# Norms without GpSimd, their roots and products in PSUM, and the squared ReLU in PSUM

## The chip, the cores and the metric

The kernel runs on one core of one Trainium2 chip. The metric is the device time of one execution in microseconds (us). Five engines matter: PE (TensorE, matmuls), DVE (VectorE), ACT (ScalarE), POOL (GpSimd) and SP (SyncE, whose queue issues all transfers). SBUF is the working memory; PSUM, eight banks of 512 fp32 columns, takes PE's results and can be read and written by DVE and ACT.

## What is computed

Two layers of a diffusion trunk work on 1024 latent tokens and 256 context tokens of width 1024. Cut to what matters here:

```python
def rmsnorm(x, g):
    y = xf * lax.rsqrt(jnp.mean(xf * xf, axis=-1, keepdims=True) + EPS)
    return y.astype(x.dtype) * g
h = rmsnorm(x, g_pre_mix) * (1 + sc1) + sh1          # "modulate"
y = concat(short conv, latent attention, conformer conv, 2-D attention)(h @ w_in) @ w_out
x = x + ga1 * rmsnorm(y, g_post_mix)                 # "norm"
hm = rmsnorm(x, g_pre_mlp) * (1 + sc2) + sh2         # "modulate"
x = x + ga2 * rmsnorm(square(relu(hm @ w1)) @ w2, g_post_mlp)   # "norm"
```

## The kernel before

Features lie on the 128 partitions (8 tiles `k`), tokens on the free axis, in three segments: 0 and 1 of 512 latent tokens, 2 of 256 context tokens. Every product is kept to fp32 accuracy by three matmuls on a high and a low part (`mm3`, L119 to L126). A weight block is loaded raw, ACT rounds it to the high part `wh`, and POOL or DVE subtracts to get the low part `wl` (L96 to L109); `walt` says how many of four go to DVE.

`rstd` (L153 to L174) makes the root of a norm: matmuls with ones sum the squares (L163), ACT takes the square root, DVE the reciprocal (L167) and a diagonal (L169), a matmul broadcasts it to all partitions (L172), and ACT copies it from PSUM into SBUF (L173). `norm` (L200 to L233) multiplies the result `y` by gain and root on DVE (L221, in place in SBUF, two SBUF inputs), adds the residual `xl` (L223: of four groups two on DVE, two on POOL), stores it, and squares and folds it (L227, L150) for the next root. `modulate` (L176 to L195) multiplies by gain and root (L188, in place), rounds the high part with its shift on ACT (L189) and makes the low part on DVE (L194), for every third `k` by an extra ACT pass and a subtraction on POOL (L191, L192).

PSUM tiles have tags: S with 3 banks, G with 2, T with 2, O with 1. A request for "R" is dealt a tag by `self.rot`: "G" means two banks turn, `ROT1 = 'SGSGS'` five, `ROT2 = 'SGSGO'` six. Attention uses S, T and O; so does the long convolution (T, O). While the attention of the later segments runs beside the first segment's MLP, `rot` is "G" (L995), and it stays so until that MLP reaches its tail and the attention is drained (L1027 to L1029).

The order of work is written out by generators: each yields a cost, and `merge` (L948) advances side work by a rate from `RATES` while the main work goes on; what is merged is issued in that order, and a scheduler with a cost model then places it on the engines' in-order queues. In `layer` (L967) the output projection of segment 1 goes in two halves, with the norm of the first half beside the second (`pn`), the norm of the second beside the context's projection (`pm`) and so on, then the MLP of segments 1 and 2. In `mlp` phase 1 makes two hidden tiles (L891, ReLU on ACT L893, square on DVE L894, high and low part), phase 2 adds eight products into the accumulators (L923).

Of the kernel before, what the change touches and what calls it, by code (L numbers as in the profile page):

```python
# [28 lines left out]
LOP = 3  # L29
PA, PB, PC, PD, PE_ = 0, 0, 1, 1, 0  # L30
DADD = (1, 3)
WALT = (3, 2)
MPE, RM, MX = 7, 1.0, 4
ROT0, ROT1, ROT2 = 'SGSGS', 'SGSGS', 'SGSGO'
# [12 lines left out]
def f32(ap):  # L47
    return ap.bitcast(F32)
# [15 lines left out]
class Kern:  # L64
# [88 lines left out]
    def rstd(self, accs, width, n, ptag, tag="e2"):  # L153
# [22 lines left out]
    def modulate(self, get, n, l, which, v, H, o, acc=None, ptag="R", tag="e2"):  # L176
# [5 lines left out]
        rs = self.rstd([acc], D, n, ptag, tag)  # L182
        yield n / 100
        A, sh = self.gains(l, "A" + which, v), self.gains(l, "s" + which, v)
        for k in range(KT):
            x = get(k)
            hi, lo = (h.k(k)[:, o:o + n] for h in (H() if callable(H) else H))
            nc.vector.scalar_tensor_tensor(x, x, A[:, k:k + 1], rs, op0=ALU.mult, op1=ALU.mult)  # L188
            nc.scalar.activation(hi, x, AF.Identity, bias=sh[:, k:k + 1])  # L189
            if k % LOP == LOP - 1:  # L190
                nc.scalar.activation(x, x, AF.Identity, bias=sh[:, k:k + 1])  # L191
                nc.gpsimd.tensor_tensor(lo, x, f32(hi), op=ALU.subtract)  # L192
            else:
                nc.vector.scalar_tensor_tensor(lo, x, sh[:, k:k + 1], f32(hi), op0=ALU.add, op1=ALU.subtract)  # L194
            yield n / 400  # L195
# [4 lines left out]
    def norm(self, y, si, o, n, l, which, acc, xsrc, xdst, nxt=None, ptag="R", tag="e2"):  # L200
# [12 lines left out]
        rs = self.rstd([acc], D, n, ptag, tag)  # L213
# [655 lines left out]
    def mlp(self, l, segs, H, atag, gtags, ends, ready=None):  # L869
# [7 lines left out]
        def phase1(b):  # L877
# [8 lines left out]
            def one(W, i, si, o, n):  # L886
# [7 lines left out]
                nc.vector.tensor_tensor(r, r, r, op=ALU.mult)  # L894
# [72 lines left out]
    def layer(self, l, H, pend):  # L967
# [45 lines left out]
        attb = ch(*[self.mla_attend(h, bsegs) for h in range(NH)], *[self.na_attend(l, h, bsegs) for h in range(NH)])  # L1013
# [263 lines left out]
```

## Time and profile before

| | us |
|---|---|
| median of 3 runs (lowest to highest) | 3301.18 (3299.84 to 3304.88) |
| profiled execution | 3295.16 |
| its span on the core | 3293.1 |
| PE busy | 2989.4 (91%) |
| DVE busy | 2150.5 (65%) |
| ACT busy | 1421.3 (43%) |
| POOL busy | 1190.5 (36%) |

The span is what the profiler's records cover; the profiled execution's own time is 2.1 us longer. Shares of busy time are averages over stages with different limits, so a stage is read by itself. TensorE's granted clock was 0.952 of full speed on the mean.

### The profile page before, as it was taken

How to read it: one execution, taken by the hardware profiler on the slowest of the kernel's cores; microseconds unless marked ns; L12 is line 12 of the kernel's file. 1: busy time of each engine (PE TensorE's matmuls, PEld its weight loads, DVE VectorE, ACT ScalarE, POOL GpSimd, SP SyncE). 2: the span in 40 equal slices, each digit the busy share in tenths (PEclk: the TensorE clock that was granted, in tenths of full speed). 3: DMA queues.
4: the chain of work that ended last, by engine and by line, in shares of the span. 5: the costliest groups of instructions: out<-in, count | busy, mean ns of one | idle time of the engine just before them, and what ended most of it. 6: DMA issues, size and time to landing. Idle time of an engine off the chain costs nothing.

```text
span 3293.1 us, 46055 instructions
## 1 busy us (share of the span) xinstructions
PE 2989.4 (91%) x15916; PEld 2552.7 (78%) x15916; DVE 2150.5 (65%) x4062; ACT 1421.3 (43%) x2933; POOL 1190.5 (36%) x927
## 2 busy tenths in 40 slices
PE   6779889879999979989999788998989999989997
PEld 5677668878877877878888577777878877877886
DVE  8999456675754487985645788557776644665445
ACT  3323455665643454213322433555665433543332
POOL 2402212234544444323333531222334444345444
PEclk9889889989999989989999899998989999999998
DMA  6435423543532354573222433425445322434233
GB/s 242 150 123 191 114 61 112 144 128 110 158 99 93 120 160 136 179 227 99 84 64 64 129 129 116 142 73 143 147 112 146 107 93 93 154 104 140 95 96 102
DMA packets 284461, 410.01 MB, mean 125 GB/s; under 512 B 28098, under 2 KB 129474, under 8 KB 284228
## 3 DMA queue, kind: packets, MB, share of 16 engines
q1 hardware_dynamic: 284228, 407.07, 40.1%
q8 instruction: 126, 2.06, 0.3%
q14 instruction: 107, 0.88, 0.1%
HBM read 354.66 MB, written 52.30 MB: 124 GB/s over the span
## 4 chain that ended last, share of the span: by engine, by line
PE 41%; DVE 12%; DMA 3%; ACT 2%; issue 2%; SPq 0%; POOL 0%; DVEq 0%; ACTq 0%; POOLq 0%
PE G L124 7%; PE G L125 7%; PE G L126 7%; PE S L124 4%; PE S L125 4%; PE S L126 4%; DMA xl<-in_wmodt_dram 2%; DVE T L400 2%; DVE xl L286 1%; PE T L673 1%; DVE ac L923 1%; DVE ac L221 1%; PE O L124 1%; PE O L125 1%; PE O L126 1%
## 5 line engine op out<-in xcount | busy, mean ns | idle before, releaser
L96 POOL TENSOR_TENSOR wl<-raw,wh 128x512 fp32r<-128x512 f32 x672 | 924.5, 1379 | 1434.5 <-ACT wh L95 1378.4
L95 ACT ACTIVATE wh<-raw 128x512 fp32r<-128x512 f32 x768 | 481.7, 629 | 798.3 <-PE G L125 357.0
L124 PE MATMUL G<-h,wh 128*128 128x512 f32 (+1 forms) x1296 | 488.9, 378 | 13.8 <-ACT wh L95 5.8
L125 PE MATMUL G<-h,wh 128*128 128x512 f32 (+1 forms) x1296 | 484.6, 374 | 5.2 <-DVE h L194 5.2
L126 PE MATMUL G<-h,wl 128*128 128x512 f32 (+1 forms) x1296 | 484.2, 374 | 2.4 <-POOL wl L96 2.4
L894 DVE TENSOR_TENSOR ge<-ge 128x512 f32<-128x512 f32 (+1 forms) x168 | 186.7, 1113 | 357.3 <-ACT ge L893 356.9
L923 DVE TENSOR_TENSOR ac<-ac,G 128x512 f32<-128x512 f32 (+1 forms) x370 | 236.8, 641 | 119.6 <-PE G L126 118.5
L124 PEld LDWEIGHTS G<-h,wh 128*128 128x128 f32 x1296 | 247.8, 191 | 58.0 <-ACT wh L95 7.1
L657 POOL TENSOR_SCALAR ah<-ah,sm 128x1280 f32<-128x1280 f32 (+3 forms) x144 | 150.0, 1045 | 380.3 <-DVE sm L656 161.6
L124 PE MATMUL G<-s,wh 128*128 128x512 f32 (+1 forms) x732 | 268.3, 368 | 17.3 <-DVE ac L923 9.1
L126 PEld LDWEIGHTS G<-h,wl 128*128 128x128 f32 x1296 | 247.7, 191 | 46.3 <-POOL wl L96 4.6
L125 PEld LDWEIGHTS G<-h,wh 128*128 128x128 f32 x1296 | 247.8, 191 | 45.8 <-DVE h L194 5.6
L126 PE MATMUL G<-s,wl 128*128 128x512 f32 (+1 forms) x732 | 261.8, 358 | 7.1 <-DVE wl L96 7.1
L125 PE MATMUL G<-s,wh 128*128 128x512 f32 (+1 forms) x732 | 261.5, 357 | 0.3 <-DVE s L96 0.3
L124 PE MATMUL S<-h,wh 128*128 128x512 f32 (+1 forms) x648 | 236.6, 365 | 3.2 <-DVE pt L96 2.6
L96 DVE TENSOR_TENSOR pt<-T,pt 128x512 fp32r<-128x512 f32 (+1 forms) x280 | 169.7, 615 | 98.7 <-ACT pt L95 97.4
L125 PE MATMUL S<-h,wh 128*128 128x512 f32 (+1 forms) x648 | 233.9, 361 | 0.0
L126 PE MATMUL S<-h,wl 128*128 128x512 f32 (+1 forms) x648 | 232.3, 359 | 1.1 <-POOL wl L96 1.1
L95 ACT ACTIVATE pt<-T 128x512 fp32r<-128x512 f32 (+1 forms) x280 | 146.7, 542 | 112.7 <-PE T L673 97.5
L673 PE MATMUL T<-ident,ah 128*128 128x128 f32 x976 | 164.8, 287 | 15.6 <-POOL ah L657 15.6
L124 PEld LDWEIGHTS G<-s,wh 128*128 128x128 f32 x732 | 139.9, 192 | 46.9 <-DVE ac L923 19.2
L400 DVE SCALAR_TENSOR_TENSOR T<-c,vec,T 128x512 f32<-128x512 f32 x240 | 169.4, 743 | 0.0
(372 smaller groups left out, 6990.8 us busy)
## 6 DMA issues: line engine op xcount, KB each, us to landing
raw<-in_w_dram SPq DMA_DIRECT2D x520, 256.0 KB, 2.6
xl<-in_wmodt_dram SPq DMA_DIRECT2D x160, 256.0 KB, 2.9
raw<-in_wout_dram SPq DMA_DIRECT2D x144, 256.0 KB, 2.9
raw<-in_win_dram SPq DMA_DIRECT2D x96, 256.0 KB, 3.1
ah<-KN SPq DMA_DIRECT2D x32, 320.0 KB, 4.7
ah<-MV SPq DMA_DIRECT2D x16, 640.0 KB, 6.4
ah<-NV SPq DMA_DIRECT2D x16, 640.0 KB, 5.2
XM<-yo SPq DMA_DIRECT2D x36, 256.0 KB, 2.7
```

What stands on the lines that cost most here:

```text
L95: nc.scalar.activation(hi, src, AF.Copy)
L96: (eng or nc.vector).tensor_tensor(lo, src, f32(hi), op=ALU.subtract)
L124: nc.tensor.matmul(out, wh, xh, start=i == 0, stop=False)
L125: nc.tensor.matmul(out, wh, xl, start=False, stop=False)
L126: nc.tensor.matmul(out, wl, xh, start=False, stop=i == last)
L221: nc.vector.scalar_tensor_tensor(yk(j), yk(j), B[:, j:j + 1], rs, op0=ALU.mult, op1=ALU.mult)
L286: nc.vector.scalar_tensor_tensor(q, w, 1.0, vecs[v][h], op0=ALU.mult, op1=ALU.mult, accum_out=dst)
L400: nc.vector.scalar_tensor_tensor(d, x, w, d, op0=ALU.mult, op1=ALU.add)
L657: nc.gpsimd.tensor_scalar(p[:, :L], p[:, :L], sm[:, 9:10], 1.0, op0=ALU.mult, op1=ALU.mult)
L673: nc.tensor.transpose(T[:, i, q * P:(q + 1) * P], ps_list[q][:, cols[q]:cols[q] + P], self.ident)
L894: nc.vector.tensor_tensor(r, r, r, op=ALU.mult)
L923: nc.vector.tensor_tensor(a, a, ps, op=ALU.add)
```

## The change

It takes the POOL instructions out of `modulate` and `norm`, so that all of their elementwise work is on DVE. `rstd` can leave its result in PSUM (`keep`, when its bank is O), and then makes no copy. With `tmp="T"` the products of L188 and L221 go to a T bank, from which the high and low parts, or the residual add, read. All norms get this but those of segment 0 beside attention, which stay in place and only lose POOL; the first segment's MLP norms and its modulates get `tmp="T"` with a rotated bank for the root. The sixth bank leaves `ROT2`. A one-step generator `turn` at the end of the attention of the later segments sets `rot` to `ROT1` as soon as that attention has been issued. In `mlp`, unless `rot` is "G", the square is written over the PSUM tile. In `layer` the norm of segment 1's first half gets the rate 1.5 in both layers (before: 0.612 in layer 0, 1.5 in layer 1) and is issued to its end before the second half's norm begins.

```diff
-ROT0, ROT1, ROT2 = 'SGSGS', 'SGSGS', 'SGSGO'
+ROT0, ROT1, ROT2 = 'SGSGS', 'SGSGS', 'SGSGS'
...
         nc.tensor.matmul(ps[:, :n], self.ones, s, start=True, stop=True)
+        if keep:
+            return ps[:, :n]
         nc.scalar.activation(s, ps[:, :n], AF.Copy)
...
-        rs = self.rstd([acc], D, n, ptag, tag)
+        rs = self.rstd([acc], D, n, ptag, tag, ptag == "O")
...
-            nc.vector.scalar_tensor_tensor(x, x, A[:, k:k + 1], rs, op0=ALU.mult, op1=ALU.mult)
-            nc.scalar.activation(hi, x, AF.Identity, bias=sh[:, k:k + 1])
-            if k % LOP == LOP - 1:
-                nc.scalar.activation(x, x, AF.Identity, bias=sh[:, k:k + 1])
-                nc.gpsimd.tensor_tensor(lo, x, f32(hi), op=ALU.subtract)
-            else:
-                nc.vector.scalar_tensor_tensor(lo, x, sh[:, k:k + 1], f32(hi), op0=ALU.add, op1=ALU.subtract)
+            t = self.ps(tmp)[:, :n] if tmp else x
+            nc.vector.scalar_tensor_tensor(t, x, A[:, k:k + 1], rs, op0=ALU.mult, op1=ALU.mult)
+            nc.scalar.activation(hi, t, AF.Identity, bias=sh[:, k:k + 1])
+            nc.vector.scalar_tensor_tensor(lo, t, sh[:, k:k + 1], f32(hi), op0=ALU.add, op1=ALU.subtract)
...
-            for j in range(k, k + g):
-                nc.vector.scalar_tensor_tensor(yk(j), yk(j), B[:, j:j + 1], rs, op0=ALU.mult, op1=ALU.mult)
             yg = y.tiles[k // y.kk][:, k % y.kk:k % y.kk + g, o:o + n]
-            (nc.vector if k // g % 4 in DADD else nc.gpsimd).tensor_tensor(yg, yg, xl, op=ALU.add)
+            t = self.ps(tmp).rearrange("p (g c) -> p g c", g=g) if tmp else yg
+            for j in range(g):
+                nc.vector.scalar_tensor_tensor(t[:, j], yg[:, j], B[:, k + j:k + j + 1], rs, op0=ALU.mult,
+                                               op1=ALU.mult)
+            nc.vector.tensor_tensor(yg, t, xl, op=ALU.add)
...
-                nc.vector.tensor_tensor(r, r, r, op=ALU.mult)
+                if self.rot == "G":
+                    nc.vector.tensor_tensor(r, r, r, op=ALU.mult)
+                else:
+                    nc.vector.tensor_tensor(ps, ps, r, op=ALU.mult)
+                    r = ps
...
-        attb = ch(*[self.mla_attend(h, bsegs) for h in range(NH)], *[self.na_attend(l, h, bsegs) for h in range(NH)])
+        attb = ch(*[self.mla_attend(h, bsegs) for h in range(NH)], *[self.na_attend(l, h, bsegs) for h in range(NH)],
+                  self.turn(ROT1))
...
-        nb = self.norm(y1, 1, 0, 256, l, "1", self.acc, xsrc, self.scr["XM"], (l, "2", HM[1]), tag="pt")
-        PB and next(nb)
-        self.merge(self.outproj(l, 1, 256, 256, y1), (nb, R['pn']))
-        n2 = self.norm(y1, 1, 256, 256, l, "1", self.acc, xsrc, self.scr["XM"], (l, "2", HM[1]), tag="pt")
-        PC and next(n2)
-        nb = ch(nb, n2)
+        free = dict(ptag="O", tag="pt", tmp="T")
+        nb = self.norm(y1, 1, 0, 256, l, "1", self.acc, xsrc, self.scr["XM"], (l, "2", HM[1]), **free)
+        self.merge(self.outproj(l, 1, 256, 256, y1), (nb, 1.5))
+        self.go(nb)
+        nb = self.norm(y1, 1, 256, 256, l, "1", self.acc, xsrc, self.scr["XM"], (l, "2", HM[1]), **free)
+        next(nb)
...
+    def turn(self, rot):
+        self.rot = rot
+        yield 0.0
```

The other norms and modulates of `layer` and `run` get `**free`, `ptag="O", tmp="T"` or `tmp="T"` alone in the same way; the last layer's second MLP norm keeps a rotated bank and gets `tmp="T"`.

## Rows read from the trace of the kernel before

**Rows 1.** The page's part 1, first line: busy time, share of the span, instructions.
```profile
PE 2989.4 (91%) x15916; PEld 2552.7 (78%) x15916; DVE 2150.5 (65%) x4062; ACT 1421.3 (43%) x2933; POOL 1190.5 (36%) x927
```
**Rows 2.** Busy time by stretch; stretch, length, engines with counts, PE clock, DMA share, GB/s.
```profile
50.00:300.00 250.00, 198.80 (x1000) 168.83 (x1001) 245.39 (x537) 77.14 (x156) 57.65 (x37) 0.90 0.42 139
...
1150.00:1265.00 115.00, 91.57 (x583) 83.65 (x582) 94.61 (x158) 62.39 (x138) 46.65 (x35) 0.90 0.48 151
1323.00:1484.00 161.00, 144.45 (x767) 125.41 (x766) 143.47 (x352) 33.78 (x64) 46.23 (x31) 0.93 0.63 203
1815.00:1940.00 125.00, 96.97 (x413) 78.45 (x412) 90.25 (x118) 61.70 (x101) 65.84 (x43) 0.88 0.43 139
...
2830.00:2925.00 95.00, 76.83 (x477) 68.43 (x476) 75.89 (x123) 48.88 (x107) 37.18 (x29) 0.91 0.42 136
```
**Rows 3.** Line L221: durations in ns, lowest/median/highest, first and last start.
```profile
L221 DVE SCALAR_TENSOR_TENSOR yo<-yo,g,pt x40: 469/476/1525, 1158.0 to 2886.9; 128x256 f32<-128x256 f32 x40
```
**Rows 4.** Groups by line and form: busy us, mean ns, idle before and releasers.
```profile
L923 DVE TENSOR_TENSOR ac<-ac,G 128x512 f32<-128x512 f32 x311 | 212.3, 683 | 112.2 <-PE G L126 111.5
...
L894 DVE TENSOR_TENSOR ge<-ge 128x512 f32<-128x512 f32 x120 | 138.6, 1155 | 355.6 <-ACT ge L893 355.3
...
L223 POOL TENSOR_TENSOR yo<-yo,xl 128x512 f32<-128x512 f32 x18 | 25.9, 1438 | 26.3 <-DVE yo L221 24.0 <-DMA xl<-in_xin_dram 2.3
...
L194 DVE SCALAR_TENSOR_TENSOR h<-x,mod,h 128x512 fp32r<-128x512 f32 x12 | 13.4, 1159 | 0.0
```
**Rows 5.** DVE in order of time: start, us, instructions; layer 0, second output projection.
```profile
1190.45 6.79 DVE L221 SCALAR_TENSOR_TENSOR yo<-yo,g,pt 128x256 f32<-128x256 f32 x8
```
**Rows 6.** PE in order of time, same stretch; in brackets the idle time before and its releaser.
```profile
1200.51 0.58 PE L126 MATMUL G<-c,wl 128*128 128x256 f32 x1 [6.91 <-DVE wl L96]
```
**Rows 7.** PE in order of time, layer 1, norm of segment 1's second half.
```profile
2881.32 0.59 PE L172 MATMUL S<-pt,ones 128*128 128x256 f32 x2
2893.96 1.02 PE L163 MATMUL S<-ones,pt 128*128 128x1 f32 x4 [9.31 <-DVE pt L150]
2900.10 0.77 PE L172 MATMUL S<-pt,ones 128*128 128x256 f32 x2
```
**Rows 8.** PE in order of time, boundary between the layers.
```profile
1849.16 0.77 PE L124 MATMUL G<-h,wh 128*128 128x512 f32 x1 [5.10 <-DVE ac L923]
...
1895.27 0.98 PE L163 MATMUL S<-ones,pt 128*128 128x1 f32 x4 [9.19 <-DVE pt L150]
```
**Rows 9.** DVE by form, 1150 to 1265 us (three norms of 256 columns).
```profile
L221 DVE SCALAR_TENSOR_TENSOR yo<-yo,g,pt 128x256 f32<-128x256 f32 x24 | 17.6, 801 | 0.9 <-ACT pt L173 0.9
...
L188 DVE SCALAR_TENSOR_TENSOR yo<-yo,g,pt 128x256 f32<-128x256 f32 x24 | 13.9, 647 | 2.1 <-ACT pt L173 2.1
L194 DVE SCALAR_TENSOR_TENSOR h<-yo,mod,h 128x256 fp32r<-128x256 f32 x17 | 10.7, 671 | 0.0
...
L223 DVE TENSOR_TENSOR yo<-yo,xl 128x512 f32<-128x512 f32 x6 | 4.5, 758 | 0.0
```
**Rows 10.** ACT in order of time: the copy of a root.
```profile
2881.95 0.38 ACT L173 ACTIVATE pt<-S 128x256 f32<-128x256 f32 x1
```
**Rows 11.** DVE in order of time: first squares of two successive MLP blocks, two stretches.
```profile
2627.55 1.41 DVE L894 TENSOR_TENSOR ge<-ge 128x512 f32<-128x512 f32 x1 [5.78 <-ACT ge L893]
...
2650.15 1.41 DVE L894 TENSOR_TENSOR ge<-ge 128x512 f32<-128x512 f32 x1 [5.77 <-ACT ge L893]
...
2999.98 1.41 DVE L894 TENSOR_TENSOR ge<-ge 128x512 f32<-128x512 f32 x1 [5.78 <-ACT ge L893]
...
3021.95 1.41 DVE L894 TENSOR_TENSOR ge<-ge 128x512 f32<-128x512 f32 x1 [5.78 <-ACT ge L893]
```
**Rows 12.** DVE in order of time: the last products of the span.
```profile
3283.30 5.27 DVE L221 SCALAR_TENSOR_TENSOR ac<-ac,g,pt 128x256 f32<-128x256 f32 x8 [1.79 <-ACT pt L173]
```
**Rows 13.** ACT and DVE in order of time: one hidden tile from ReLU to low part.
```profile
3246.57 0.58 ACT L893 ACTIVATE ge<-G 128x512 f32<-128x512 f32 x1
...
3249.28 0.69 DVE L96 TENSOR_TENSOR ah<-ge,ah 128x512 fp32r<-128x512 f32 x1
```

More of the change, by code (lines that the diff above doesn't have):

```diff
@@ L172, in rstd, with modulate @@
         nc.tensor.matmul(ps[:, :n], self.ones, s, start=True, stop=True)
+        if keep:
+            return ps[:, :n]
         nc.scalar.activation(s, ps[:, :n], AF.Copy)
         return s
-    def modulate(self, get, n, l, which, v, H, o, acc=None, ptag="R", tag="e2"):
+    def modulate(self, get, n, l, which, v, H, o, acc=None, ptag="R", tag="e2", tmp=None):
         nc = self.nc
@@ L198, in newh, with norm @@
         return tuple(Seg(self.pools[tag], n, F32R, tag, self.nm("h")) for _ in range(2))
-    def norm(self, y, si, o, n, l, which, acc, xsrc, xdst, nxt=None, ptag="R", tag="e2"):
+    def norm(self, y, si, o, n, l, which, acc, xsrc, xdst, nxt=None, ptag="R", tag="e2", tmp=None):
         nc = self.nc
@@ L232, in norm @@
             yield n / 200
-            yield from self.modulate(yk, n, l2, w2, v, H, o, acc, ptag, tag)
+            yield from self.modulate(yk, n, l2, w2, v, H, o, acc, ptag, tag, tmp)
     def mod_pe(self, load):
@@ L1050, in layer @@
             HM[2] = self.newh(256)
-            nb = self.norm(y2, 2, 0, 256, l, "1", self.acc, xsrc, self.scr["XM"], (l, "2", HM[2]), tag="pt")
-            PE_ and next(nb)
+            nb = self.norm(y2, 2, 0, 256, l, "1", self.acc, xsrc, self.scr["XM"], (l, "2", HM[2]), **free)
         self.merge(m0, (nb, R['pt']))
-        resa = self.norm(acc0, 0, 0, 512, l, "2", None, self.scr["XM"], xout)
+        resa = self.norm(acc0, 0, 0, 512, l, "2", None, self.scr["XM"], xout, tmp="T")
         self.walt = 0
@@ L1061, in layer @@
             self.go(resa)
-            nb = self.norm(self.macc[1], 1, 0, 256, l, "2", None, self.scr["XM"], xout, tag="pt")
+            nb = self.norm(self.macc[1], 1, 0, 256, l, "2", None, self.scr["XM"], xout, **free)
             self.stats(nb)
-            n2 = self.norm(self.macc[1], 1, 256, 256, l, "2", None, self.scr["XM"], xout, tag="pt")
+            n2 = self.norm(self.macc[1], 1, 256, 256, l, "2", None, self.scr["XM"], xout, tag="pt", tmp="T")
             self.go(m)
@@ L1082, in hn @@
             HN[0] = self.newh(512)
-            yield from self.modulate(get0, 512, 1, "1", 0, HN[0], 0)
+            yield from self.modulate(get0, 512, 1, "1", 0, HN[0], 0, tmp="T")
         hn = hn()
@@ L1087, in layer @@
         self.go(nb, hn)
-        p1 = self.norm(self.macc[1], 1, 0, 512, l, "2", None, self.scr["XM"], xout, (1, "1", lambda: HN[1]), tag="pt")
+        p1 = self.norm(self.macc[1], 1, 0, 512, l, "2", None, self.scr["XM"], xout, (1, "1", lambda: HN[1]), **free)
         self.stats(p1)
@@ L1091, in layer @@
         HN[1], HN[2] = self.newh(512), self.newh(256)
-        pend = ch(p1, self.norm(self.macc[2], 2, 0, 256, l, "2", None, self.scr["XM"], xout, (1, "1", HN[2]), tag="pt"))
+        pend = ch(p1, self.norm(self.macc[2], 2, 0, 256, l, "2", None, self.scr["XM"], xout, (1, "1", HN[2]), **free))
         return HN, pend
+    def turn(self, rot):
+        self.rot = rot
+        yield 0.0
     @staticmethod
@@ L1159, in early @@
             load(0, "ah")
-            g = self.modulate(X[0].k, 512, 0, "1", 0, lambda: H[0], 0)
+            g = self.modulate(X[0].k, 512, 0, "1", 0, lambda: H[0], 0, tmp="T")
             self.stats(g)
@@ L1170, in run @@
         self.go(first[0])
-        pend = self.chain(*[self.modulate(X[si].k, SEGS[si][1], 0, "1", int(si == 2), H[si], 0) for si in (1, 2)])
+        pend = self.chain(*[self.modulate(X[si].k, SEGS[si][1], 0, "1", int(si == 2), H[si], 0, ptag="O", tmp="T") for si in (1, 2)])
         H, pend = self.layer(0, H, pend)
```

8 lines of the change are left out of this document (3 added, 5 removed).

## The prediction

> **What bounds the kernel now.** I read the busy times first: PE works 91% of the span [rows 1], so only stretches in which it waits can give much. Next the busy time by stretch: three stretches lie well under that share, and all three hold norms that stand between two matmul stages. They are the later output projections of layer 0 (1150 to 1265 us: PE 91.6 of 115), the boundary of the layers (1815 to 1940: 97.0 of 125) and the same projections in layer 1 (2830 to 2925: 76.8 of 95). PE idles 23.4 + 28.0 + 18.2 = 69.6 us in them, and its granted clock was 0.90, 0.88 and 0.91, while DVE works 72 to 82% of the time. Two more stretches are DVE's: the start (245.4 of 250) and the stage in which layer 1's modulation rows run beside the MLP (143.5 of 161) [rows 2].
>
> Then one line by its spread. The norm's product L221, 256 columns with both inputs in SBUF, takes 476 ns at the median and up to 1525 [rows 3]. The MLP's square of SBUF by itself averages 1155 ns, while an add of the same shape with one input from PSUM averages 683 over 311 instructions; a POOL add of that shape takes 1438 [rows 4]. I read it so: a DVE instruction with two SBUF inputs stands still while a POOL instruction beside it reads SBUF, and one with an input in PSUM doesn't. In layer 0 a burst of eight products lasts 6.79 us where 8 x 0.476 = 3.8 would do [rows 5], and a low weight part queued behind it lets PE wait 6.91 us [rows 6]. In layer 1 PE waits 9.31 us at the second root of a norm for the folded squares: 12.6 us go by between the broadcast of the first root and the sum of the second [rows 7]. At the boundary it waits 5.10 us for an accumulation queued behind such products and 9.19 us for squares [rows 8]. So these stretches are set by the norms' chain on DVE.
>
> **The change part by part.**
>
> *Norms of 256 columns, layer 0.* In 1150 to 1265 us three norms with their modulates take on DVE 17.6 (24 products), 13.9 (24), 10.7 (17 low parts, so 11.3 for 18) and 4.5 us (6 adds) [rows 9], together 47.3. After it, 24 products, 24 products and 24 low parts each have an operand in PSUM. Undisturbed a product lasts 0.476, and in a burst neighbours overlap: 17.6 us for 24 x 0.801 is a factor 0.92, so 0.436 each and 31.4 for 72. Twelve adds at 0.68 make 8.1. DVE saves 47.3 - 39.5 = 7.8 us, although it takes over POOL's work. Besides, one POOL add a norm stands between a product and its square: 3 x (1.44 - 0.68) = 2.3. All of it is on the path, since PE waits for it. I take 10; bounds 3 (the low weight parts on DVE stay disturbed by POOL's) and 15 (the 6.91 us of wait goes as well).
>
> *The same in layer 1 and at the boundary.* Two norms make 2/3 of it: 7, bounds 2 to 10. The boundary has one norm of 512 columns and one of 256, as much as three: 10, bounds 3 to 18, the two waits and half of the rest.
>
> *The copies of the root* go in these seven norms and their seven modulates: 14 x 0.38 = 5 [rows 10]; bounds 2 and 6.
>
> *One O bank, two T banks.* Here the change adds waits. A norm's root now waits until the modulate before it has read its root from O; before, it had a bank of its own. Behind that sum of squares in PE's queue stand the projection's matmuls. From sum to broadcast took 6.14 us [rows 7]; four times a norm follows a modulate (twice in layer 0, once in layer 1, once at the boundary), and I charge half, 12 us. In a modulate the third product must wait until ACT and DVE have emptied the first T bank. The trace doesn't show that; nearest are the products, which now save time, and it is in the same bound: 0 to -20. The rate 1.5 issues the second root earlier in layer 0, as layer 1 does already; nothing is charged.
>
> *Clock.* In the three stretches PE is busy 265 us at some 0.90, so about 27 us are clock. 10 + 7 + 10 + 5 = 32 of 69.6 us idle go, 46%; the same share of 27 is 12. Bounds 3 and 18.
>
> *Five banks for the end of the first segment's MLP.* Under "G" a block of that MLP takes 2650.15 - 2627.55 = 22.60 us; with rotated banks the same work in layer 1's last MLP takes 21.97 [rows 11]. The switch now comes with the end of attention, eight blocks earlier in layer 1 and as many in layer 0: 16 x 0.63 = 10. Bounds 0 (the switch has no effect) and 10.4.
>
> *Start.* DVE is full there, so its time counts: 12 low parts of 512 columns take 13.4 us; 16 (four come from POOL) at 0.683 take 10.9. Gain 2.5, bounds 0 and 5.
>
> *Tail.* Eight products take 5.27 us at the end [rows 12], then 3.5; two POOL adds move to DVE, 1.4. With the earlier half: 1, bounds 0 and 3.
>
> *Squared ReLU.* In PE-bound stretches DVE is half idle; what it saves there costs and gives nothing while the bank is free in time (rival two). Where DVE is full (modulation rows) I take 2, bounds -10 and 5. Segment 0's norms beside attention stay in SBUF: two adds and two low parts more on DVE against as much less disturbance, 0, bounds -4 and 4. The sixth bank is lost, but a G or O bank came round every fifth request before as it does now: 0.
>
> Sum: 10 + 7 + 10 + 5 - 12 + 12 + 10 + 2.5 + 1 + 2 = 47.5. The profiled execution took 3295.2, so 3247.7; the median of the runs shown is 6.0 higher: 3253.7, and I say 3253.
>
> [...] By the rows an operand in PSUM costs DVE nothing: 0.683 us for 512 columns [rows 4]. [...] The sum goes by the rows.
>
> **Rivals.**
>
> *One: the chain is only moved.* The single O bank and the turn of two T banks give back what the products save, and only the banks of the MLP (10), the tail (1) and the start (2.5) remain: 3301.2 - 13.5 = 3288. For it: norms now run strictly one after the other. Against it: DVE has less work, POOL much less, and PE's longest waits name DVE's queue.
>
> *Two, the slower side: the square holds its bank.* Before, a hidden tile's bank was free after ReLU; now after square, high and low part. Between two uses of a bank lie four other tiles; in phase 2 a tile is 6 of 96 matmuls of a block, 21.97/16 = 1.37 us, so 5.5 us are allowed. From ReLU's start at 3246.57 to the low part's end at 3249.97 it took 3.4 us, with the slow square in it [rows 13]. If it held 7 us, PE would stand 1.5 us at each of some 46 block ends (15 + 15 + 16), 69 us, and 47.5 less of gain leave 3323. It decides from 47.5/46 = 1.0 us over, a hold of 6.5 us; against it is that the 3.4 leave room, for it only DVE's full queue beside the modulation rows.
>
> *Three: the switch doesn't come.* If attention is issued to its end only where the MLP reaches its tail, the 10 us are lost: 3263.
>
> *Four: dearer PSUM operands.* The most that the rows leave open is what the fastest and the median product differ by, 476 - 469 = 7 ns [rows 3]; on some 250 moved instructions that is 2 us, 3255. [...]
>
> **How the numbers follow.** What a measurement of this kernel can tell from no change is 0.2%, 6.6 us. Forecast with its sizes off either way 0.66; rival one 0.20; rival two 0.06; three 0.04; four 0.04. The low bounds of most terms together come near rival one, the high ones to some 80 us of gain; all of them at once is unlikely, so the range goes from 3215 to 3290 and takes in rivals one and three. Rival one lies 13.5 us under the time before, and a quarter of it would fall within 6.6: faster 0.66 + 0.04 + 0.04 + 0.15 = 0.89, same 0.05, slower 0.06.
>
> **What would show it.** Right: products L221 and L188 of the later segments near 0.48 us at the highest too; PE's waits for squares in the three stretches cut by a third or more; blocks of 22.0 us as soon as attention ends. Wrong: new PE waits at the sum of squares for the O bank as long as the old ones; PE waits for the low part of a hidden tile at the ends of blocks; DVE bursts in modulate broken up by ACT.

## The result, and the profile after

The changed kernel takes 3201.85 us (median of 4 runs, 3193.89 to 3206.12) against 3300.51 (3288.22 to 3304.88): a ratio of 0.9708, 95% interval 0.969 to 0.9725. It is faster by 98.7 us; 48 were forecast, with a range that ended at 3215. The profiled execution took 3201.57 us, its span is 3199.6, so 93.5 us less than the span before. The direction was right and the size was not: by spans, 46 us more came than the 47.5 of the forecast's sum. Where from?

The busy times first, the first line of the page of after (compare [rows 1]).

```profile
PE 2959.4 (92%) x15916; PEld 2534.7 (79%) x15916; DVE 2019.0 (63%) x4128; ACT 1399.5 (44%) x2882; POOL 1076.6 (34%) x861
```

POOL lost 114 us and 66 instructions, and DVE, which took these over, lost 131 us as well. PE does the same 15916 matmuls and is busy 30 us less, at a mean granted clock of 0.961 instead of 0.952.

Next I cut both traces at marks that every kernel has: the first transpose of a layer's attention (on PE, into T) and the starts of the ReLUs, numbered 0 to 167, on ACT. In the table, "forecast" shares out the forecast's terms: the copies by the number of norms and modulates, the O charge by its four places, the clock by the idle time of the three stretches. One profiled execution stands behind each time.

| stretch | before | after | gain | forecast |
|---|---|---|---|---|
| start to layer 0's first transpose | 378.6 | 370.1 | 8.5 | 2.5 |
| attention, to ReLU 0, to ReLU 16 | 559.8 | 561.5 | -1.7 | 0 |
| ReLU 16 to 32 (five banks, layer 0) | 182.1 | 174.3 | 7.8 | 5 |
| ReLU 32 to 70 (later projections, modulation rows) | 436.5 | 425.8 | 10.7 | 12.2 |
| ReLU 70 to 99 | 239.7 | 239.4 | 0.3 | 0 |
| **ReLU 99 to layer 1's first transpose (boundary)** | 307.8 | 266.6 | **41.2** | 13.3 |
| attention of layer 1, to ReLU 118 | 545.0 | 539.6 | 5.4 | 0 |
| ReLU 118 to 133 (five banks, layer 1) | 163.9 | 159.3 | 4.6 | 5 |
| ReLU 133 to 150 (later projections, layer 1) | 251.8 | 237.0 | 14.8 | 8.6 |
| ReLU 150 to the end | 227.8 | 225.9 | 1.9 | 1 |

The boundary makes 28 of the 46 missing us, the projections of layer 1 and the start 6 each, and 5 lie in layer 1's attention, which the change hardly touches. These are the windows around the three stretches of norms, cut at equal matmul work; columns as in [rows 2]. First the kernel before:

```profile
1140.00:1290.00 150.00, 126.57 (x829) 116.19 (x828) 114.59 (x189) 79.62 (x177) 59.12 (x45) 0.92 0.45 139
1811.00:1950.00 139.00, 110.97 (x513) 92.04 (x512) 102.37 (x138) 64.51 (x108) 70.03 (x46) 0.89 0.41 133
2820.00:2940.00 120.00, 101.83 (x627) 90.72 (x626) 85.94 (x136) 63.74 (x137) 50.49 (x38) 0.93 0.43 139
```

And the kernel after:

```profile
1124.50:1263.00 138.50, 121.44 (x825) 112.07 (x824) 105.88 (x207) 73.64 (x163) 41.66 (x32) 0.91 0.48 154
1784.70:1886.40 101.70, 101.31 (x516) 85.86 (x515) 73.36 (x124) 55.17 (x93) 51.44 (x36) 1.00 0.54 182
2743.00:2853.30 110.30, 98.19 (x629) 89.47 (x628) 74.10 (x144) 60.64 (x129) 39.02 (x30) 0.94 0.47 151
```

At the boundary PE's idle time fell from 28.0 us to 0.4, and its granted clock rose from 0.89 to 1.00, so that the same matmuls take 101.3 us instead of 111.0. No idle time is left in this window. What PE waited for there, before (1811 to 1950):

```profile
PE S L163 <- DVE pt L150: 18.5, 3, 9.2
PE G L124 <- DVE ac L923: 5.1, 1, 5.1
PE G L124 <- ACT wh L95: 3.4, 1, 3.4
```

And after (1784.7 to 1886.4; L161 is L163 of before, L148 is L150):

```profile
PE O L161 <- DVE pt L148: 0.4, 1, 0.4
```

The waits for squares [rows 8] are gone. In layer 1 one remains that is as long as the 9.31 us of [rows 7]; it is the fourth sum there, right behind the broadcast of the root before (which is recorded as two matmuls), with nothing between:

```profile
2811.45 0.59 PE L170 MATMUL O<-pt,ones 128*128 128x256 f32 x2
2821.97 0.99 PE L161 MATMUL O<-ones,pt 128*128 128x1 f32 x4 [9.92 <-DVE pt L148]
```

In layer 0's projections a wait of this length is new. There PE waited 10.2 us for low weight parts and 3.6 us for squares before; now the low parts are in time, and 8.7 us pass at the fourth sum, again with no matmul between it and the broadcast (1124.5 to 1263):

```profile
PE O L161 <- DVE pt L148: 8.7, 1, 8.7
```

The products of 256 columns of the later segments (norm L223, modulate L192), which reached 1525 ns in [rows 3], by their spread:

```profile
L223 DVE SCALAR_TENSOR_TENSOR T<-yo,g,O x40: 472/479/490, 1142.9 to 2818.6; 128x256 f32<-128x256 f32 x40
L192 DVE SCALAR_TENSOR_TENSOR T<-yo,g,O x40: 473/481/490, 1165.4 to 2831.1; 128x256 f32<-128x256 f32 x40
```

### The profile page after: what moved, and what is told of

The parts are those of the page before. It is cut to its first block, busy times and chain, and to the rows that moved or that the text cites. A ratio compares the mean times of both kernels' runs of the same rounds, so it can differ in the third digit from the quotient of the medians.

```text
span 3199.6 us, 46244 instructions
## 1 busy us (share of the span) xinstructions
PE 2959.4 (92%) x15916; PEld 2534.7 (79%) x15916; DVE 2019.0 (63%) x4128; ACT 1399.5 (44%) x2882; POOL 1076.6 (34%) x861
## 4 chain that ended last, share of the span: by engine, by line
PE 70%; DVE 9%; DMA 5%; ACT 2%; issue 2%; SPq 1%; POOL 0%; DVEq 0%; ACTq 0%; POOLq 0%
PE G L122 11%; PE G L123 11%; PE G L124 11%; PE S L122 9%; PE S L124 9%; PE S L123 9%; PE T L675 3%; DMA xl<-in_wmodt_dram 2%; PE O L688 1%; PE O L687 1%; DVE xl L288 1%; DMA ah<-KR 1%; PE S L809 1%; PE S L758 1%; PE S L759 1%
## 5 line engine op out<-in xcount | busy, mean ns | idle before, releaser
L122 PE MATMUL G<-h,wh 128*128 128x512 f32 (+1 forms) x1128 | 427.0, 379 | 6.5 <-ACT h L193 2.3
L123 PE MATMUL G<-h,wh 128*128 128x512 f32 (+1 forms) x1128 | 423.0, 375 | 4.4 <-DVE h L194 4.3
L122 PE MATMUL S<-h,wh 128*128 128x512 f32 (+1 forms) x904 | 324.6, 359 | 2.9 <-ACT h L193 1.6
L124 PE MATMUL S<-h,wl 128*128 128x512 f32 (+1 forms) x904 | 324.7, 360 | 1.4 <-POOL wl L94 1.4
L123 PE MATMUL S<-h,wh 128*128 128x512 f32 (+1 forms) x904 | 323.7, 358 | 0.0
L929 DVE TENSOR_TENSOR ac<-ac,S 128x512 f32<-128x512 f32 (+1 forms) x340 | 208.9, 617 | 114.6 <-PE S L124 113.7
L122 PEld LDWEIGHTS G<-h,wh 128*128 128x128 f32 x1128 | 215.7, 191 | 46.0 <-ACT h L193 4.7
L123 PEld LDWEIGHTS G<-h,wh 128*128 128x128 f32 x1128 | 215.2, 191 | 42.2 <-DVE h L194 6.0
L929 DVE TENSOR_TENSOR ac<-ac,G 128x512 f32<-128x512 f32 (+1 forms) x268 | 169.0, 631 | 82.1 <-PE G L124 80.9
L122 PEld LDWEIGHTS S<-h,wh 128*128 128x128 f32 x904 | 173.9, 192 | 29.5 <-ACT h L193 2.3
L124 PEld LDWEIGHTS S<-h,wl 128*128 128x128 f32 x904 | 173.6, 192 | 27.3 <-POOL wl L94 2.7
L123 PEld LDWEIGHTS S<-h,wh 128*128 128x128 f32 x904 | 173.9, 192 | 25.6
L122 PE MATMUL G<-s,wh 128*128 128x512 f32 (+1 forms) x534 | 185.3, 348 | 2.2 <-ACT ge L863 1.7
L124 PE MATMUL G<-s,wl 128*128 128x512 f32 (+1 forms) x534 | 182.0, 341 | 3.3 <-DVE wl L94 3.2
L123 PE MATMUL G<-s,wh 128*128 128x512 f32 (+1 forms) x534 | 182.0, 341 | 0.3 <-DVE s L94 0.3
```

The costliest lines, as they stand in the source:

```text
L122: nc.tensor.matmul(out, wh, xh, start=i == 0, stop=False)
L123: nc.tensor.matmul(out, wh, xl, start=False, stop=False)
L124: nc.tensor.matmul(out, wl, xh, start=False, stop=i == last)
L929: nc.vector.tensor_tensor(a, a, ps, op=ALU.add)
```

## Experiments

Medians of whole runs carry a disturbance that has to be known. An edit anywhere makes the scheduler order the rest differently, and the attention of layer 1 (first transpose to ReLU 101, then to 118) came out between 317 and 333 us and between 219 and 228 in kernels whose edits lie elsewhere. So I read an edit in its own stretch, and take a difference of whole runs under 10 us for nothing by itself. The other stretches move less, but they move too. In the kernels made from the changed one that leave a stretch's own code alone, the start took 367.2 to 373.1 us, ReLU 32 to 70 421.1 to 425.9 and the boundary 266.6 to 276.7 (changed kernel: 370.1, 425.8 and 266.6). A difference inside such a spread is not shown. All ratios are to the kernel before, which had medians of 3294.5 to 3296.3 beside these runs, 4 to 6 us under the one beside the changed kernel; so a loss told against 3201.85 us is some 4 to 6 us too small.

The expectations weigh two theories. Theory A: POOL and products with two SBUF inputs slow the norms' chain on DVE. Theory B: what counts is how many other matmuls may stand ahead of a sum of squares in PE's queue.

### The boundary, taken apart

Four kernels put back parts of the boundary's norms and modulates (`p1` and `pend` in `layer`) in the changed kernel.

All back, POOL too; `pool=True` restores the lines that the change removed:

```diff
-... (1, "1", lambda: HN[1]), **free)
+... (1, "1", lambda: HN[1]), tag="pt", pool=True)
-... (1, "1", HN[2]), **free))
+... (1, "1", HN[2]), tag="pt", pool=True))
```

> The changed kernel, with the two norms and two modulates at the layer boundary put back as they were before: products in SBUF, a rotated bank for the root with its copy, two of eight (or four) adds and every third low part on POOL. Set side by side at equal matmul work, the boundary (1811 to 1950 us of the kernel before) is 37 us shorter in the changed kernel, against the 10 forecast. If that gain is made by the boundary's own norms, all of it is lost: 3202 + 37 = 3239 us, with PE waiting some 18 us for folded squares there again. If it comes from what stands before or beside them (fewer squares and adds on DVE in the MLP, the sixth bank gone), at most 15 us are lost: 3217 or less.

3232.18 us (ratio 0.9812, 0.9797 to 0.9826).

As before, but without POOL:

```diff
-... (1, "1", lambda: HN[1]), **free)
+... (1, "1", lambda: HN[1]), tag="pt")
-... (1, "1", HN[2]), **free))
+... (1, "1", HN[2]), tag="pt"))
```

> As the kernel with the boundary put back, but without POOL: products in SBUF, root in a rotated bank with its copy, all adds and low parts on DVE. Theory A (POOL's reads hold up DVE, and its adds stand in the chain): most of the 37 us stay, 3212 us or less. Theory B (what counts is where the sums of squares stand in PE's queue, which the O and T banks moved back): sums stand early again, PE waits 15 us or more for squares, 3225 to 3239 us.

3227.24 us (0.9794, 0.978 to 0.9809).

Roots in turning banks, products in T:

```diff
-... (1, "1", lambda: HN[1]), **free)
+... (1, "1", lambda: HN[1]), tag="pt", tmp="T")
-... (1, "1", HN[2]), **free))
+... (1, "1", HN[2]), tag="pt", tmp="T"))
```

> The changed kernel, but at the layer boundary the roots lie in rotated banks and are copied to SBUF; products stay in T. My forecast charged the single O bank 12 us for four norms, a quarter of it here: 3 us would be gained and four copies of 0.4 to 0.6 us lost, 3200 to 3202 us. Theory A: the products stay fast, 3202 to 3207 us. Theory B, if it is the O bank that orders the sums: 10 to 20 us are lost, 3212 to 3222 us.

3224.05 us (0.9782, 0.9767 to 0.9796).

Roots in O, products in SBUF:

```diff
-... (1, "1", lambda: HN[1]), **free)
+... (1, "1", lambda: HN[1]), ptag="O", tag="pt")
-... (1, "1", HN[2]), **free))
+... (1, "1", HN[2]), ptag="O", tag="pt"))
```

> The changed kernel, but at the layer boundary the products lie in SBUF, in place; the roots stay in O without a copy, and POOL stays out of the norms. Theory A in its form for PSUM operands: a product has one operand in PSUM still (the root), so products of 512 columns stay near 0.75 us, only low parts and adds read SBUF twice; 3205 to 3212 us. Theory B, if it is the turn of two T banks that breaks up the bursts of products: bursts of eight return, accumulations and squares stand behind them, 3212 to 3230 us.

3216.6 us (0.976, 0.9744 to 0.9776); 4.5 us of the loss lie at the boundary, 11 in layer 1's attention. After these four, the missing corner, POOL and SBUF, but roots in O:

```diff
-... (1, "1", lambda: HN[1]), **free)
+... (1, "1", lambda: HN[1]), ptag="O", tag="pt", pool=True)
-... (1, "1", HN[2]), **free))
+... (1, "1", HN[2]), ptag="O", tag="pt", pool=True))
```

> The changed kernel with the boundary's four norms and modulates as before (products in SBUF, POOL's adds and low parts), but their roots in O, without copy. It fills the square of the boundary runs: from the last ReLU of layer 0 to the first transpose of layer 1's attention the stretch is 296.7 us with turning banks and POOL, 291.3 with turning banks and no POOL, 271.1 with O and no POOL, 266.6 with O, no POOL and T. If O and POOL add up, it is 271.1 + 5.4 = 276.5 us here, and the run 3210 to 3217 us. If POOL's part counts only once the sums stand further back, it is 285 us or more, and the run 3220 to 3230 us.

3205.8 us (0.9731, 0.9711 to 0.9751). The stretch itself:

| root | products | POOL in the norms | stretch, us | sum 4 behind |
|---|---|---|---|---|
| turning | SBUF | yes (b_all_back) | 296.7 | 264 |
| turning | SBUF | no (b_no_pool_only) | 291.3 | 264 |
| turning | T | no (b_root_turns) | 289.4 | 264 |
| O | SBUF | yes (d_pool_and_o) | 270.1 | 399 |
| O | SBUF | no (b_in_place) | 271.1 | 396 |
| O | T | no (after) | 266.6 | 353 |

The last column counts in the timeline the matmuls of `mm3` that PE does between the last one that reads the long segment's hidden tiles and the fourth sum of squares. The root in O is worth 20 to 27 us in every pair of rows. POOL makes 5.4 with turning banks and nothing with O, T 2 to 4.5; both lie inside the spread of 10 us of an untouched boundary. So theory A by itself does not make the boundary, and the sum that I expected for d_pool_and_o (276.5) did not come: with O, POOL's share is gone as well. But O stands for two things in these rows, since a root in O is also read from PSUM, without a copy. The 32 products of the boundary take 26.4 us together in b_root_turns and 19.7 in the changed kernel. A run that moves the bank alone follows below (c_o_bank_alone). Waits of PE in 1775 to 1960 us of b_all_back:

```profile
PE G L161 <- DVE pt L148: 9.5, 1, 9.5
PE S L161 <- DVE pt L148: 7.1, 1, 7.1
PE S L122 <- ACT wh L93: 4.8, 1, 4.8
```

And of d_pool_and_o, with the same POOL work:

```profile
PE O L161 <- DVE pt L148: 3.6, 2, 2.8
```

With turning banks the fourth sum stood behind exactly 264 matmuls in all three kernels; with O it stands behind 353 to 399. The sum itself comes little earlier: 110.5 to 121.3 us after ReLU 99 with turning banks, 106.5 to 119.1 with O. So PE does more work while DVE makes the squares. Over the whole boundary it idles 32 to 37 us with turning banks and 15 to 18 with O, and its granted clock was 0.92 to 0.94 and 0.97 to 0.98. Why the turn limits the order is argued from the code, not shown by itself: a root holds a bank from its sum to its copy (in b_all_back 4 to 9 us up to its broadcast alone), and the tile that is dealt this bank next can't start before, nor pass the sum in PE's queue; so at most the tiles of the other banks lie between. No other tile of this stretch asks for O.

### The same bank in the kernel before

O out of the turn of six, nothing else:

```diff
-ROT0, ROT1, ROT2 = 'SGSGS', 'SGSGS', 'SGSGO'
+ROT0, ROT1, ROT2 = 'SGSGS', 'SGSGS', 'SGSGS'
```

> The kernel before with O taken out of the turn of six banks, and nothing else. Against it stands the run that also puts the boundary's roots into O (3302 us; boundary 289.9 us, hidden tiles 36 to 70 of layer 0 296.8 us). If the lost bank costs the MLP 4 us and gives the boundary nothing, this one is 3296 to 3302 us with a boundary of 306 to 309 us, and O was worth 18 us there. If freeing O from the turn is itself what shortens the boundary, the boundary is 290 to 300 us here. The forecast's term for the sixth bank is 0: 3295 us.

3308.58 us (1.0043, 1.0025 to 1.0061). Boundary 307.4 us: freeing O gives nothing there. ReLU 32 to 70 takes 445.5 us instead of 436.5: the sixth bank was worth 9 us, where my term said 0.

The same, and the boundary's roots in O; their copies, POOL and the SBUF products stay:

```diff
-... (1, "1", lambda: HN[1]), tag="pt")
+... (1, "1", lambda: HN[1]), ptag="O", tag="pt")
-... (1, "1", HN[2]), tag="pt"))
+... (1, "1", HN[2]), ptag="O", tag="pt"))
```

> The kernel before with one edit: the roots of the two norms and two modulates at the layer boundary go to bank O (with their copy to SBUF), and O leaves the turn of the MLP banks. Products stay in SBUF, POOL keeps its work. Theory B (a root outside the turning banks lets more matmuls stand ahead of the next sum): most of the 22 us that its loss cost in the changed kernel come here too, 3294 - 15 to 25 = 3269 to 3279 us, and the stretch from the MLP's last hidden tile to the first matmul of the keys and values falls from 115.6 us to 90 to 100. Forecast's term (a root that waits for O is a cost, 3 us here): 3297 us. Theory A (POOL and SBUF operands make the stretch): no change, 3290 to 3297 us.

3302.1 us (1.0019, 1.0004 to 1.0033). As a whole none of the three theories; in its stretch theory B: 289.9 us, 17.5 less than with five banks. Layer 1's attention gave 16 of them back (332.7 to ReLU 101 instead of 317.1), the disturbance told of above. Here the copies stay, and the 32 products are no faster (33.8 us against 32.0), so this is the bank by itself. It is also the plainest case for theory B. The fourth sum comes 126.1 us after ReLU 99 in both kernels, but behind 264 matmuls with five banks and 362 with the roots in O:

```profile
1810.61 0.37 ACT L893 ACTIVATE ge<-G 128x256 f32<-128x256 f32 x1
1936.73 1.01 PE L163 MATMUL S<-ones,pt 128*128 128x1 f32 x4 [7.53 <-DVE pt L150]
```

```profile
1807.38 0.36 ACT L893 ACTIVATE ge<-G 128x256 f32<-128x256 f32 x1
1933.46 0.92 PE L163 MATMUL O<-ones,pt 128*128 128x1 f32 x4 [2.93 <-DVE pt L150]
```

PE's waits in 1800 to 1960 us with five banks alone:

```profile
PE S L163 <- DVE pt L150: 16.5, 3, 7.5
PE G L124 <- DVE pt L96: 5.1, 1, 5.1
PE G L124 <- DVE ac L923: 5.1, 1, 5.1
```

And with the roots in O:

```profile
PE O L163 <- DVE pt L150: 5.8, 2, 2.9
PE O L172 <- DVE pt L169: 3.8, 1, 3.8
```

Then all later roots, with the same edit in three more calls:

```diff
-... (l, "2", HM[1]), tag="pt")
+... (l, "2", HM[1]), ptag="O", tag="pt")
...
-... (l, "2", HM[2]), tag="pt")
+... (l, "2", HM[2]), ptag="O", tag="pt")
```

> The kernel before with one thing: all roots of the later norms (those of 256 columns after the output projections, and the boundary's) go to bank O, with their copies, and O leaves the turn of six. Products in SBUF, POOL as before, squares in SBUF, no earlier switch. Against the kernel before with five banks alone (3308.6 us): if the root's bank acts by itself, the boundary gains 18 us (289.9 against 307.4), the 256-column norms of both layers another 13 and 7: 3265 to 3278 us. If it needs the shorter chain or the new order of the norms, 3295 to 3305 us.

3281.54 us (0.9956, 0.9944 to 0.9969): 27 us under the run with five banks, 14 under the kernel before. The boundary takes 288.6 us, ReLU 133 to 150 246.2 instead of 251.7, ReLU 32 to 70 444.2 instead of 445.5. So the bank acts by itself, less than in the changed kernel; in layer 0's projections its 1.3 us show nothing.

### The 256-column norms in the changed kernel

Their roots back in turning banks, products in T:

```diff
-... (l, "2", HM[1]), **free)
+... (l, "2", HM[1]), tag="pt", tmp="T")
...
-... (l, "2", HM[2]), **free)
+... (l, "2", HM[2]), tag="pt", tmp="T")
```

> The changed kernel, but the norms of 256 columns after the output projections, in both layers, have their roots in turning banks with a copy; their products stay in T. The forecast's term says that the single O bank costs 9 us for the three of its four places that lie here, against 2 to 4 us for the copies: 3195 to 3198 us. If O lets matmuls stand ahead of the sums here too, as at the boundary, 3206 to 3216 us.

3221.16 us (0.9777, 0.9757 to 0.9797). ReLU 32 to 70 lost 2.3 us, 133 to 150 7.2, the boundary, whose roots stayed in O, 10.1. Then all later roots, this edit and that of b_root_turns together:

> The changed kernel with every root of the later norms in turning banks again, with copies: those of 256 columns in both layers and the boundary's. Products stay in T, POOL stays out, squares and the earlier switch stay. By halves it cost 19.3 us (256 columns) and 22.2 us (boundary). If the two add up, 3243 us. If the halves share what they cost, as the 256-column run's own loss of 10 us at the boundary hints, 3225 to 3235 us. The forecast's term (O costs 12, copies 5 saved) would have 3195 us.

3237.4 us (0.9822, 0.9806 to 0.9839): 35.5 us, less than the sum of 41.5. 21.6 lie at the boundary, 1.2 and 1.4 in the projections, 15 in layer 1's attention. The same edit in layer 1's projections thus cost 7.2 us once and 1.4 once, so for the 256-column norms a root in O is worth 1 to 7 us, not a cost of 9. At the boundary the fourth sum stood behind 310 matmuls in this run, not 264, but PE waited 6.9 us at the second sum: the count at one sum is a sign of the order, not a measure of the time.

### Products, POOL, and the start

All elementwise work as before, roots in O:

```diff
-    def norm(..., ptag="R", tag="e2", tmp=None):
+    def norm(..., ptag="R", tag="e2", tmp=None, pool=True):
...
-free = dict(ptag="O", tag="pt", tmp="T")
+free = dict(ptag="O", tag="pt")
```

and so for `modulate` and in every call with `tmp="T"`.

> The changed kernel with its O roots, five banks, turn and order, but with all elementwise work of all norms and modulates as before: products in SBUF, in place, adds and every third low part on POOL. At the boundary alone this cost 3.5 us (270.1 against 266.6). If the root's bank makes the change, the whole is 3205 to 3222 us: the 256-column stretches lose 2 to 5 us each and the start up to 8.5. If POOL and SBUF operands are what made the later projections' stretches, the start and the tail long (my reading of the trace before), 40 us or more come back: 3240 us or more.

3230.86 us (0.9814, 0.9785 to 0.9843). Start +5.3, ReLU 32 to 70 +6.4, boundary +6.4, ReLU 133 to 150 +8.8. Then without POOL, only the products in place:

```diff
-free = dict(ptag="O", tag="pt", tmp="T")
+free = dict(ptag="O", tag="pt")
```

and `tmp="T"` removed from the other calls.

> The changed kernel with all products of norms and modulates in SBUF, in place, but without POOL in them; roots in O. With POOL's adds and low parts back as well it was 3230.9 us. If POOL's share of the norms made that, 3202 to 3212 us here; if it is the SBUF operands of DVE, which low weight parts on POOL still stop, or the two T banks that put product, add and square in turn, 3222 to 3231 us.

3232.87 us (0.981, 0.9796 to 0.9825): +3.1, +11.6, +3.3 and +2.3 in the same stretches, and 11 in layer 1's attention. The first lies between the two cases that I had written down, the second just above its upper one. By the medians the products' place makes the 29 us and POOL nothing; by the stretches it is not so plain: in layer 1's projections it is POOL (8.8 against 2.3), in layer 0's the products' place (11.6 without POOL, 6.4 with it), at the boundary and at the start both runs stay in or near the spread, and the second run owes a third of its loss to the order in attention. The products themselves say it better, spread over 40 of 256 columns each. Roots copied to SBUF, products into T, no POOL in the norms (f_all_roots_turn):

```profile
L223 DVE SCALAR_TENSOR_TENSOR T<-yo,g,pt x40: 478/484/1525, 1142.6 to 2849.7; 128x256 f32<-128x256 f32 x40
```

Root read from O, product in place in SBUF, no POOL (f_in_place_everywhere):

```profile
L223 DVE SCALAR_TENSOR_TENSOR yo<-yo,g,O x40: 470/473/480, 1146.5 to 2842.3; 128x256 f32<-128x256 f32 x40
```

The same with POOL in the norms (e_pool_everywhere, where the line is L227), and a low part with two SBUF inputs beside it:

```profile
L227 DVE SCALAR_TENSOR_TENSOR yo<-yo,g,O x40: 471/477/481, 1152.1 to 2837.5; 128x256 f32<-128x256 f32 x40
L198 DVE SCALAR_TENSOR_TENSOR h<-yo,mod,h x54: 461/476/1516, 684.8 to 2855.9; 128x256 fp32r<-128x256 f32 x54
```

So the root left in PSUM is what frees the products; T as their output does not. Whether POOL works at that moment can be read from the traces. In the kernel before, 23 of the 80 in-place products of this shape in norm and modulate took over 600 ns, and a POOL instruction ran during each of them; the 37 with no POOL instruction beside them took 486 ns at most. In f_all_roots_turn it is 19 of 27 with POOL beside them and none of 53 without. With the root in PSUM (e_pool_everywhere), 54 of 80 had POOL beside them, and none took over 481.

The start's modulates with products in SBUF and roots in turning banks:

```diff
-g = self.modulate(X[0].k, ..., lambda: H[0], 0, tmp="T")
+g = self.modulate(X[0].k, ..., lambda: H[0], 0)
-... H[si], 0, ptag="O", tmp="T") for si in (1, 2)])
+... H[si], 0) for si in (1, 2)])
```

> The changed kernel, but the three modulates of the start have their products in SBUF, in place, and their roots in rotated banks with a copy; POOL stays out. The forecast's term for the start was 2.5 us, by the low parts alone: 3204 us. By the traces the start is 11 us shorter in the changed kernel; if products in PSUM and the roots in O make it, 3209 to 3214 us; if the absence of POOL makes it, 3200 to 3204 us.

3228.65 us (0.9801, 0.9787 to 0.9816), a miss: but the start itself lost 1.0 us, and the rest is order in attention (9.9 us in ReLU 0 to 16, 14.7 in layer 1) and 4.3 at the boundary. So neither O nor T is shown to make the start's 8.5 us. With POOL back 5.3 of them were lost (e_pool_everywhere), 2.3 us beyond the spread of the start: POOL is the likely part, and the rest is not placed. DVE's rows of 0 to 250 us, before:

```profile
L194 DVE SCALAR_TENSOR_TENSOR h<-x,mod,h 128x512 fp32r<-128x512 f32 x12 | 13.4, 1159 | 0.0
...
L150 DVE TENSOR_TENSOR e<-e,e 128x256 f32<-128x256 f32 x7 | 9.1, 1303 | 0.0
```

After (0 to 240):

```profile
L194 DVE SCALAR_TENSOR_TENSOR h<-T,mod,h 128x512 fp32r<-128x512 f32 x16 | 11.6, 732 | 0.0
...
L148 DVE TENSOR_TENSOR e<-e,e 128x256 f32<-128x256 f32 x7 | 5.5, 785 | 0.0
```

Four more low parts take 1.8 us less, and seven folds that nothing in the change touches 3.6 us less. The folds are luck: each of the five long ones before (0.9 to 2.9 us) ran beside a low part that POOL makes in L96 (four of weights, one of `ah`), none beside POOL's part of a modulate, and in f_in_place_everywhere, where POOL has no part in modulates either, the seven take 8.4 us.

### Switch and square

No earlier switch:

```diff
-attb = ch(..., self.turn(ROT1))
+attb = ch(...)
```

> The changed kernel without the switch to five banks at the end of attention. The forecast's term says 16 blocks x 0.63 = 10 us, so 3212 us; by the aligned traces the hidden tiles 16 to 32 of the first MLPs gained 7.8 and 4.7 us, 3214 us. With the old switch the squares of these blocks go back to SBUF as well; if only that counted, 3205 us or less. Rival three (the switch has no effect): 3202 us.

3220.21 us (0.9777, 0.9758 to 0.9795). ReLU 16 to 32 takes 183.0 us again and 118 to 133 163.9, 8.7 and 4.6 more: the 13 that the traces gave. The squares, which went back to SBUF with the switch, have no part in it: with squares in SBUF alone (c_square_sbuf, next) the same tiles take 174.6 and 159.3 us. The rest of the loss lies in attention and the boundary.

Square in SBUF everywhere:

```diff
-if self.rot == "G":
-    nc.vector.tensor_tensor(r, r, r, op=ALU.mult)
-else:
-    nc.vector.tensor_tensor(ps, ps, r, op=ALU.mult)
-    r = ps
+nc.vector.tensor_tensor(r, r, r, op=ALU.mult)
```

> The changed kernel with the square of the ReLU in SBUF everywhere. By the reading of the two traces, the stage with layer 1's modulation rows (hidden tiles 36 to 60 of layer 0) is 8 us longer in the changed kernel, and PE waits 15.5 us there for the low part of a hidden tile, which now holds its bank. If that is the square's doing, this kernel gains 4 to 8 us: 3194 to 3198 us. If those waits only took the place of others (the five waits of 15.2 us for accumulations that stood there before), it is the same within 3 us; if the square in SBUF slows DVE where it is needed, 3205 to 3212 us.

3208.54 us (0.9742, 0.9725 to 0.9758): no gain; ReLU 32 to 70 is 2.2 us longer. Rival two's wait is there, it only took another's place. PE's waits among the modulation rows, before (1290 to 1510 us):

```profile
PE G L124 <- DVE ac L923: 15.2, 5, 5.5
```

After (1263 to 1483.5):

```profile
PE G L122 <- DVE c L94: 15.5, 4, 5.7
```

### Three attempts to go further

Layer 0's second MLP with six banks until its last block:

```diff
-ROT0, ROT1, ROT2 = 'SGSGS', 'SGSGS', 'SGSGS'
+ROT0, ROT1, ROT2 = 'SGSGS', 'SGSGS', 'SGSGO'
...
-self.rot = ROT2
+self.rot = ROT1 if last else ROT2
...
+self.rot = ROT1
 p1 = self.norm(...)
```

> The changed kernel, but layer 0's second MLP has O in its turn of six until its last block's first half is done, then five. In the kernel before, the lost sixth bank cost the hidden tiles 36 to 70 5.8 us (298.2 against 292.4). If that is so here too, 3194 to 3198 us. If the roots of the norm beside it, which now lie in O, are held up by the tiles, or the tiles by them, 3202 to 3212 us.

3202.7 us (0.9721, 0.9695 to 0.9748); ReLU 32 to 70 425.9 against 425.8: nothing. Two more roots in O:

```diff
-resa = self.norm(acc0, ..., tmp="T")
+resa = self.norm(acc0, ..., ptag="O", tmp="T")
...
-yield from self.modulate(get0, ..., HN[0], 0, tmp="T")
+yield from self.modulate(get0, ..., HN[0], 0, ptag="O", tmp="T")
```

> The changed kernel, but two more roots of 512 columns go to O and lose their copy: the residual norm of segment 0 and the modulate of segment 0 for layer 1, both beside the second MLP, among the modulation rows. If a root in a turning bank stops the order there as well, the hidden tiles 36 to 70 (297.6 us) gain 3 to 8 us: 3194 to 3199 us, with layer 1's 140 to 150 alike. If PE has matmuls enough there in any case, it is the same within 3 us.

3213.87 us (0.9756, 0.9731 to 0.9781); 424.9 us there, nothing, and 6.6 us lost at the boundary. Fewer low weight parts on DVE:

```diff
-WALT = (3, 2)
+WALT = (3, 1)
```

> The changed kernel, but at the later output projections only one of four low weight parts is made on DVE instead of two, and POOL, which the norms no longer use, makes the rest. In the changed kernel PE still waits 8.7 and 9.9 us for folded squares on DVE there (layers 0 and 1), and DVE makes 22 and 17 such parts in these stretches, 17.1 and 11.7 us. If DVE's queue sets these waits, a third to a half of that work leaves it: 3190 to 3197 us. If the low parts on POOL come too late for the matmuls (1.34 us each against 0.78), 3202 to 3210 us.

3219.75 us (0.977, 0.9751 to 0.9789): 0.1 us in ReLU 32 to 36, 3.4 lost in 133 to 150, the rest in attention. The longest waits for squares are still 8.7 and 9.3 us, so DVE's low parts don't set them. No version is faster than the changed kernel.

## Why the forecast was wrong

**The step that failed is "One O bank, two T banks", -12 us.** I took the O bank for a new wait: a root that waits until another has been read, with the projection's matmuls behind it. The runs show the opposite sign: 20 to 27 us gained at the boundary with the roots in O (17.5 by the bank alone, in the kernel before), 1 to 7 in the projections. I had read PE's waits at the sums as DVE being late. They are as much PE being without other work: with the bank alone moved, the fourth sum came at the same time and PE had done 98 more matmuls by then. That the turn of banks sets this limit is the reading of the code. My rows showed the sums in S, a bank of the turn [rows 7], and I didn't ask which tiles the root's bank held up. The term also stands for most of "layer boundary", where I let 46% of the idle time go; all of it went.

**Layer boundary**, forecast 10 (13.3 with its shares), bounds 3 to 18 before clock: 41.2 measured. POOL and T, which the term was made of, give 3.5 with O and some 7 with turning banks (296.7 to 289.4), less than an untouched boundary varies by; nothing shows the 10. 11 of the 41 us are still open: b_all_back takes 296.7 us where the kernel before takes 307.8, though its boundary is as before; square, bank turn (307.4) or earlier work were not separated, and it is hardly more than that spread.

**Norms of 256 columns**: layer 0 12.2 forecast, 10.7 measured; layer 1 8.6 and 14.8. The elementwise work made 6.4 and 8.8 of these by e_pool_everywhere, near 10 and 7 (11.6 and 2.3 by f_in_place_everywhere, so these sizes are rough); the charge for O was wrong in both. The new order of the two halves' norms was put back in no run. **Copies**, 5 forecast: every run that put them back moved the root as well, so no run shows this term.

**Clock**: 12 forecast. PE's busy time fell by 5.1, 9.7 and 3.6 us in the three windows, together 18.4, but not all of it is clock. At the boundary the granted clock went from 0.89 to 1.00. In layer 0's projections it went from 0.92 to 0.91, so it can't have made the 5.1, and in layer 1's from 0.93 to 0.94, some 1 us of the 3.6. By this estimate the clock gave near 11 us, nearly all at the boundary and not shared out by idle time as I had it; what made the other 8 is open.

**Five banks**: 10 forecast, 12.4 measured, 13.3 by c_no_turn; right. The sixth bank, costed at 0, was worth 9 us in the kernel before (445.5 against 436.5); in the changed kernel it is worth none (425.9 against 425.8).

**Start**: 2.5 forecast, 8.5 measured. The low parts gave 1.8 us of DVE's time as I read it. The folds' 3.6 us came by luck, and the rest is open.

**Squared ReLU and tail**: +2 and +1 forecast. The square gives 2.2 us in its stretch and 6.7 in the whole run, within the spread of order; the tail 1.9.

**Sources in PSUM**: the sum let them cost DVE nothing, by the rows, and that held. Low parts of 256 columns in the changed kernel, from T and from SBUF:

```profile
L194 DVE SCALAR_TENSOR_TENSOR h<-T,mod,h 128x256 fp32r<-128x256 f32 x56 | 25.2, 477 | 3.3 <-ACT h L193 2.5
...
L194 DVE SCALAR_TENSOR_TENSOR h<-yo,mod,h 128x256 fp32r<-128x256 f32 x32 | 13.5, 474 | 0.0
```

3 ns, 250 times, is under 1 us.

**The rivals**: one (the chain is only moved), three (no switch) and four (dear operands) didn't happen; two's wait came, at no cost. Of what I said would show it, products at 0.48 to 0.49 us and blocks of 21.8 us (174.3 / 8) came. At O stand a wait of 9.92 us in layer 1, in the old one's place, and a new one of 8.7 us in layer 0; both are for folded squares, not for the bank.

## What to carry to other kernels

A small result that lives long, such as a norm's root, can cost more than its size if it takes a bank of the turn that feeds the matmuls: here 17.5 to 27 us at the boundary, where PE had other work to do, 1 to 7 in the projections, and nothing among the modulation rows (e_more_o_roots). The price shows as a wait for some other engine. Before costing a wait, ask both what makes the awaited work late and what else the waiting engine could do meanwhile. Read an edit in its own stretch, between marks that all kernels share; the whole time carries changes of order elsewhere of up to 16 us. And before calling a difference shown, see how much the same stretch varies where its code is the same.

## What the runs showed of the hardware

A norm's DVE product of 256 columns with two SBUF inputs took up to 1525 ns, against 484 at the median, even with its output in PSUM and the norms off POOL (f_all_roots_turn). Of norm's and modulate's products of this shape there, 19 took over 600 ns, all of them with a POOL instruction beside them; in the kernel before it was 23, also all with one. With one input in PSUM, such a product took 481 ns at most, in place in SBUF and with POOL at work beside 54 of the 80 (e_pool_everywhere). I had expected that a product with any operand in PSUM goes undisturbed; an output there didn't help.
